# A hybrid decoder block: four instead of three k pairs by seven products in the second groups of two down parts

## The chip, the core and the metric

The kernel runs on one core of one Trainium2 chip. The core has a matrix engine (PE, with a separate weight-load stage PEld), a vector engine (DVE), an activation engine (ACT), a general engine (POOL) and a queue engine for transfers (SP). Each engine works through its own instructions in the order in which they stand; between engines only semaphores order anything. Weights come from the chip's memory by transfers that SP issues, and some by transfers that POOL issues and that add to what already lies in the buffer.

The metric is the device time of one execution in microseconds (us).

## The reference

One decoder layer over 256 tokens of width 2048 in float32: a Griffin branch and a stick-breaking attention side by side, a gated merge, then a SwiGLU feed-forward part and a gated per-layer embedding. Only the feed-forward part is touched here:

```python
h = rmsnorm(x, g_ffn[i])
gu = h @ w_ffn_gu[i]
g, u = jnp.split(gu, 2, axis=-1)
x = x + (jax.nn.silu(g) * u) @ w_ffn_down[i]
```

`w_ffn_gu` is 2048 by 11264 and `w_ffn_down` 5632 by 2048. The change concerns the last product, the down projection.

## The kernel before

**Products.** Everything is computed in float32 quality from operands that are split into a high and a low part of a format that the matrix engine takes. One product of a 128x128 token tile with a 128x512 weight tile is therefore three matmuls (high by high, high by low, low by high), written out in `prod` (L656; its matmuls are L658, L659, L660). The 256 tokens are two tiles. Weights are split after they have landed: ACT writes the high part `whi` (L374), DVE the low part `wlo` (L375). There are five buffers for each (pool `phl`, L432), so that a piece of weights can be split only when PE is through with the piece five places before it.

**Stages.** The feed-forward part runs as 11 gate-up groups `gu` (L1258) and three down parts `dn0`, `dn1`, `dn2` (`down`, L1291), interleaved: gu 0 to 3, dn0, gu 4 to 7, dn1, gu 8 to 10, dn2. A down part takes the k tiles that the groups before it have made (16, 16 and 12 of the 44) and has two groups, g = 0 and g = 1, one for each half of the 2048 output columns. Each group is two column blocks of 512 by two token tiles, and each adds its result onto the residual `x1`. Both groups of a part use the same tokens: the gated activations `acts`, one buffer for each pair of k tiles.

**Seven products for eight.** Two neighbouring k tiles (a pair), two token tiles and two column blocks make a 2x2 by 2x2 block product. Done plainly, it takes eight products (four for each k tile, an integer in the slot list). Done by Winograd's form of Strassen's scheme it takes seven, at the price of sums of weights and sums of tokens. The slot lists at L25 to L34 fix in which order the pieces of a group come. The first two such pairs share slots with string names ("11", "T1", "21", "T2", "22", "T3", "T4"); a third and a fourth pair have slots of their own, `A1`..`A4` = ("S", i, 2) and `B1`..`B4` = ("S", i, 3). `EVEN3` has three pairs by seven products and ten k tiles plainly; `EVEN4` has four pairs and eight k tiles plainly:

```python
EVEN3 = ["11", A1, 6, "T1", A2, 7, "21", 8, "T2", 9, "22", A3, 10, "T3", 11, A4, 12, "T4", 13, 14, 15]
EVEN4 = ["11", A1, 8, B1, "T1", 9, A2, B2, 10, "21", "T2", 11, "22", A3, 12, B3, "T3", 13, A4, B4, 14, "T4", 15]
```

`products` (L66) says how many products a slot has: four for an integer, two for a string name and for i = 1, 2, 3 of a third or fourth pair, one for i = 4. The gate-up groups (except the first) run `EVEN4`, dn0 and dn1 run `EVEN3` in both groups, dn2 has a list of its own.

**Sums of weights.** `Stream.summed` (L291) makes them on DVE (L296) just before a piece is split. For a third or fourth pair the piece ("S", 2) needs two adds of 128x512 into a new buffer, called Y here: Y's left half is the sum of a half of the pair's S1 buffer and a half of its S2 buffer, Y's right half is that plus the other half of S2. The piece "T2" needs one add of 128x1024, of the raw piece "22" into the running sum R. Other sums are made by POOL's adding transfers (`joins`, L330; L334). The raw pieces lie in 128x1024 buffers of the pool "Q" (31 of them, L437), from which the activations, the token sums and the norm-scaled inputs come as well; the plain k tiles have four buffers of their own (`p32`).

**Sums of tokens.** `half_sums` (L662) makes four sums of a pair's quarters on DVE (128x128 each) and splits them into a Q buffer (ACT copy, DVE subtract); with `defer` the split is put on a list that `group` runs at a slot. For gu outputs this is done in `turn` (L1270) while the pair is turned. Which pairs get sums is decided by `pairs_of` (L53): three for dn0 and dn1, so pairs 0 to 2 and 8 to 10. `parts_sums` (L970) makes the sums of a pair later, from its high and low parts; the value inputs of the attention and the attention output use it.

**Order.** `group` (L729) writes the products slot by slot, keeps a running time (0.68 for a product) at which `run_todo` starts work that was put off, such as the adds onto `x1` (`ends_x1` and `onto_x1`, L1188 to L1202), and calls `also[n]` at slot n. `Stream.need` (L387) lets the transfers, the splits and the sums run ahead. The order of the transfers on SP is planned by `dma_order` (L223) from the slot lists. After that a scheduler places each engine's instructions, and the pool gives out the buffers in the order of the program; a transfer or a sum that writes a buffer waits for the last reader of what lay in it before.

Of the kernel before, what the change touches and what calls it, by code (L numbers as in the profile page):

```python
# [29 lines left out]
FQ = [16, 16, 12]  # L30
FQ0 = [0, 16, 32]
# [4 lines left out]
EVEN3 = ["11", A1, 6, "T1", A2, 7, "21", 8, "T2", 9, "22", A3, 10, "T3", 11, A4, 12, "T4", 13, 14, 15]  # L36
EVEN4 = ["11", A1, 8, B1, "T1", 9, A2, B2, 10, "21", "T2", 11, "22", A3, 12, B3, "T3", 13, A4, B4, 14, "T4", 15]
LONG = ["11", 8, A1, 9, B1, "T1", 10, A2, 11, B2, "T2", 12, "21", 13, "22", A3, 14, B3, "T3", 15, A4, 16, B4, 17, "T4",
        18, 19, 20, 21]
TWELVE = [("S", 1, 0), ("S", 1, 1), 4, ("S", 2, 0), 5, ("S", 2, 1), 6, ("S", 3, 0), 7, ("S", 3, 1), 8, ("S", 4, 0), 9,  # L40
          ("S", 4, 1), 10, 11]
# [126 lines left out]
def tail():  # L168


    def wide(name, w, slots, c=0):
        return [(name, g, w, c + 8 * g, c + 8 * g + 4, slots[g]) for g in range(2)]

    def blocks(*cs):
        return [("blk", b, None, c, None, None) for c, b in cs]

    def gu(*gs):
        return [("gu", g, "gu", 4 * g, 44 + 4 * g, EVEN4 if g else FIRST3) for g in gs]

    def dn(q):  # L180
        k, p = FQ0[q], FQ0[q] // 2
        slots = [x + k if isinstance(x, int) else (*x[:2], x[2] + p) if isinstance(x, tuple) else x
                 for x in (EVEN3 if FQ[q] == 16 else TWELVE)]
        return wide(f"dn{q}", "dn", [slots] * 2)

    x = [("x", 0), ("x", 1)]
    return (wide("ro", "ro", [LONG] * 2) + wide("v", "in", [EVEN4] * 2, C_V)
            + [("qk", b, "in", C_Q + 4 * b, C_K + 4 * b, EVEN4) for b in range(2)]
            + blocks(*[(c, b) for b in (2, 3) for c in (C_Q, C_K)], *[(C_GTA, b) for b in range(4)])
            + wide("ao", "ao", [EVEN3] * 2) + wide("wo", "wo", [FIRST3, EVEN3]) + gu(0, 1, 2, 3) + dn(0) + gu(4, 5, 6, 7) + dn(1)  # L190
            + gu(8, 9, 10) + dn(2)
            + wide("pg", "pg", [FIRST3[:-4] + x + FIRST3[-4:]] * 2))
# [234 lines left out]
def tile_hybrid_block(ctx: ExitStack, tc: tile.TileContext, xT: bass.AP, x: bass.AP, pT: bass.AP,  # L427
# [12 lines left out]
    def tl(tag, dt=F32):  # L440
        cnt[0] += 1
        tag = "H" if tag in "CT" else "Q"
        n, c = NT[tag]
        return act.tile([P, c], dt, tag=tag, name=f"{tag}_{cnt[0]}", bufs=n)
# [217 lines left out]
    def half_sums(h, defer=False):  # L662


        a11, a21, a12, a22 = (h[:, c * P:c * P + P] for c in range(4))
        q = tl("T")
        s1, s2, s3, s4 = (q[:, c * P:c * P + P] for c in range(4))
        tt(s1, a21, a22, ALU.subtract)
        tt(s2, s1, a11, ALU.subtract)
        tt(s3, a11, a21, ALU.subtract)  # L670
        tt(s4, a12, s2, ALU.add)
        t = tl("X", F32R)

        def in_parts():
            actv(t[:, :512], q, AF.Copy)
            tt(t[:, 512:], q, f32(t[:, :512]), ALU.subtract)

        if defer:
            deferred.append(in_parts)
        else:  # L680
            in_parts()
        return [(t[:, c * P:c * P + P], t[:, 512 + c * P:640 + c * P]) for c in range(4)]
# [46 lines left out]
    def group(at, pairs, sums, after=None, also=()):  # L729

        name, g = at
        slots = [x for n, y, _, _, _, sl in HEAD + TAIL if (n, y) == at for x in sl
                 if isinstance(x, int) or is_sum(x)]
        turned_at = TURNED_AT["twelve" if len(slots) == len(TWELVE) else
                              "first" if slots[2] == 6 and slots[8] == "22" else "even"]  # L740
        seq = [(n, q, 0, 512) for n, x in enumerate(slots) for q in products(x, pairs_of(name)[:2])]
        if at == LAST_GROUP:
            k = len(slots) - 4
            rest = [q for q in seq if q[0] >= k]
            seq = [q for q in seq if q[0] < k] + [q for b in "243" for q in rest if q[1][0] == b]
            seq += [(n, (b + f, *q), e, e + 256) for e, f in ((0, "a"), (256, "b")) for n, (b, *q), _, _ in rest
                    if b == "8"]
        first, last = {}, {}
        for i, (_, (b, y, _, _), e, _) in enumerate(seq):
            first.setdefault(b, i)  # L750
            last[b, e] = i
            if y in ("11", "T1", "T2", "T3"):
                last[y] = i
        banks, tile_, got = {}, {}, {}
        begin = [0.0]
        for x in slots:
            begin.append(begin[-1] + 0.68 * len(products(x)))
        turns = list(turned_at)
        for i, (n, (b, y, p, c), e0, e1) in enumerate(seq):
            if n not in got:  # L760
                if n in also:
                    also[n]()
                run_todo(begin[n])
                while deferred:
                    with behind_splits():
                        deferred.pop(0)()
                if pend and turns and n >= turns[0] and not any(x[2] for x in todo):
                    turns.pop(0)
                    with tc.issue_after(mm_.ins):
                        pend.pop(0)()  # L770
                got[n] = S_.take(("tok", name, g, slots[n]))
            if b not in banks:
                banks[b] = psum()
            ps = banks[b]
            if p is None:
                o = tok(pairs, *y)
            else:
                o = {"11": tok(pairs, 2 * p, 0), "21": tok(pairs, 2 * p + 1, 0), "22": sums[p][3],
                     "T1": sums[p][0], "T2": sums[p][1], "T3": sums[p][2],
                     "T4": tok(pairs, 2 * p + 1, 1)}[y]  # L780
            _, _, hi, lo, w0 = got[n].columns(c)
            s = slice(w0 + e0, w0 + e1)
            mm_ = prod(ps[:, e0:e1], o, hi[:, s], lo[:, s], i == first[b], i in (last[b, e0], last.get(y)),
                 b == "B")
            if y in ("11", "T1", "T2", "T3") and i == last[y]:
                t = tile_[y] = tl("T")
                with tc.issue_after(S_.hi_ins.ins):
                    actv(t, ps, AF.Copy)
                if y == "T3":
                    with tc.issue_after(S_.lo_ins.ins):  # L790
                        tt(tile_["T2"], tile_["T1"], tile_["T2"], ALU.subtract)
                        tt(tile_["T1"], tile_["T1"], t, ALU.subtract)
                    if after is not None:
                        after(tile_, begin[n])
        run_todo(1e9)
        tile_["ends"] = [banks[b] for b in ("8a", "8b") if b in banks]
        return [banks[b] for b in "2438"], tile_
# [105 lines left out]
    @contextmanager  # L903
    def behind_splits():
        with tc.issue_after(S_.hi_ins.ins), tc.issue_after(S_.lo_ins.ins):
            yield
# [11 lines left out]
    also = {max(1, 2 * i - 4): [later(next_xg)] for i in range(2, NPD)}  # L918
    for i in range(NPD):
        also.setdefault(2 * i + 1 if i < 7 else 14, []).append(squares_x(i))  # L920
    also = {n: (lambda fs: lambda: [f() for f in fs])(fs) for n, fs in also.items()}
# [45 lines left out]
            later_on(a if tied else 0.0, (lambda c, q: lambda: tt(c, q, c, ALU.add))(c, q), True, tied)  # L967
        return cs

    def parts_sums(pairs, sums, p):  # L970
        h = tl("T")
        hi, lo = parts(pairs[p])
        tt(pair(h), f32(hi), f32(lo), ALU.add)
        sums[p] = half_sums(h)

    def last_gate():
        with behind_splits():
# [7 lines left out]
    for g in range(2):  # L985
        also = {n - 4 + i: (lambda p: lambda: parts_sums(xg, xsum, p))(p) for i, p in enumerate(pairs_of("v"))} if g else {
            8: last_gate, 12: next_table}
# [200 lines left out]
    def onto_x1(g):  # L1188

        def run(tiles, at):  # L1190
            for n, c in enumerate(("11", "T3", "T2", "T1")):
                o = x1[n % 2][2 * g + n // 2]
                later_on(at + 1.3 + 2.7 * n, (lambda o, t: lambda: tt(o, o, t, ALU.add))(o, tiles[c]), False)
        return run

    def ends_x1(pss, g, i):

        for n, ps in enumerate(pss):
            t, b = n % 2, 2 * g + n // 2
            later_on(max(0.0, JOINS_AT[n] - 1.3), (lambda o, ps: lambda: tt(o, ps, o, ALU.add))(x1[t][b], ps), True, n > 1)  # L1200
            if i is not None:
                later_on(6.8 + 2.7 * n, (lambda t, b: lambda: squares(i, t, b))(t, b), False)  # L1202
# [52 lines left out]
    acts, asum = {}, {}  # L1255
# [32 lines left out]
        pend.extend(turn(f) for f in range(2))  # L1288

    def down(q, g):  # L1290
        ends_x1(group((f"dn{q}", g), acts, asum, onto_x1(g))[0], g, 1 if q == 2 else None)  # L1291
        if q == 2:
            for p in range(4 * g, 4 * g + 4):
                pend.append(next_h(h3, sum3, p, PC_GP))
# [114 lines left out]
```

## Time and profile before

| | before |
|---|---|
| median of 3 runs (us) | 1850.68 (1850.08 to 1850.79) |
| profiled execution (us) | 1850.56 |
| its span (us) | 1848.9 |
| PE busy in the span | 1839.4 us, 99% |
| DVE busy | 1536.1 us, 83% |
| ACT busy | 1269.5 us, 69% |
| granted PE clock | full (1.0) |

The profile's first part gives for each engine the time in which it was busy. PE's busy time is modelled: matmuls overlap, so a row's duration (0.39 us for 128x512) is longer than the step from one matmul to the next. Idle time of PE is time in which it stood for want of an operand. In the lists, a row names a source line, an engine, an operation and the tiles (out<-in); "idle before" is how long the engine had nothing to do ahead of it, and the name behind the arrow is what ended that. The lines of helpers stand for many places: L374 and L375 are every split of a piece of weights, L454 and L460 are DVE's and ACT's general helpers.

### The profile page before, as it was taken

The page shows a single profiled execution, that of the slowest core. Times are in us where ns is not written, and L with a number is a line of the kernel's source. Part 1 is how long each engine was busy: PE and PEld are TensorE (multiplying, and loading weights), DVE is VectorE, ACT ScalarE, POOL GpSimd, SP SyncE. Part 2 cuts the span into 40 slices and gives each one's busy share as a digit, 9 for nine tenths or more (in the row PEclk, how much of TensorE's full clock was granted, in tenths as well). Part 3 has the DMA queues.
Part 4 walks back from the last instruction along what each step waited for, and adds up shares of the span by engine and source line. Part 5 has one row for each costly group of instructions (what it writes and reads, how often), then busy time and mean ns, then how long its engine had stood idle before and what let it go on. Part 6 is the DMA issues. An engine that isn't in the chain of part 4 may idle for free.

```text
span 1848.9 us, 24803 instructions
## 1 busy us (share of the span) xinstructions
PE 1839.4 (99%) x8855; PEld 1547.3 (84%) x8855; DVE 1536.1 (83%) x1940; ACT 1269.5 (69%) x1705; POOL 129.5 (7%) x156
## 2 busy tenths in 40 slices
PE   9999999999999999999999999999999999999998
PEld 7899899888888888888888888888888888888787
DVE  7688888677899977667799889888899888898987
ACT  7587888775566777776656686665566665666675
POOL 0000000010011100000000011100111101111100
PEclk9999999999999999999999999999999999999999
DMA  8555556587788855456788778888888888887774
GB/s 291 181 177 186 185 195 194 199 257 247 243 259 237 250 176 168 152 160 218 232 239 256 222 245 247 249 252 239 265 255 251 229 241 245 253 259 225 206 249 131
DMA packets 123388, 414.37 MB, mean 224 GB/s; under 512 B 13824, under 2 KB 14464, under 8 KB 123264
## 3 DMA queue, kind: packets, MB, share of 16 engines
q1 hardware_dynamic: 101808, 359.82, 55.5%
q0 software_dynamic: 21312, 52.96, 17.0%
q8 instruction: 69, 1.13, 0.2%
q14 instruction: 55, 0.45, 0.1%
q10 hardware_dynamic: 144, 0.01, 0.0%
HBM read 410.64 MB, written 2.10 MB: 223 GB/s over the span
## 4 chain that ended last, share of the span: by engine, by line
PE 97%; DVE 2%; issue 0%; ACT 0%; ACTq 0%
PE ps L658 26%; PE ps L659 26%; PE ps L660 26%; PE ps L576 9%; PE ps L580 5%; PE ps L559 1%; PE ps L560 1%; PE ps L558 1%; DVE wlo L375 1%; DVE H L454 1%; PE ps L1277 1%; PE ps L1035 0%; DVE Q L296 0%; PE ps L1222 0%; PE ps L495 0%
## 5 line engine op out<-in xcount | busy, mean ns | idle before, releaser
L659 PE MATMUL ps<-wlo,Q 128*128 128x512 f32 x2175 | 848.8, 390 | 1.3 <-DVE wlo L375 1.3
L660 PE MATMUL ps<-whi,Q 128*128 128x512 f32 x2175 | 845.7, 389 | 0.0
L658 PE MATMUL ps<-whi,Q 128*128 128x512 f32 x2175 | 751.5, 391 | 0.6 <-ACT whi L374 0.4
L375 DVE TENSOR_TENSOR wlo<-w,whi 128x1024 fp32r<-128x1024 f32 (+2 forms) x478 | 575.3, 1208 | 172.3 <-ACT whi L374 167.8
L374 ACT ACTIVATE whi<-w 128x1024 fp32r<-128x1024 f32 (+2 forms) x478 | 497.4, 1047 | 216.1 <-PE ps L660 168.1
L374 ACT ACTIVATE whi<-Q 128x1024 fp32r<-128x1024 f32 (+1 forms) x377 | 376.6, 1004 | 231.2 <-PE ps L660 184.3
L375 DVE TENSOR_TENSOR wlo<-Q,whi 128x1024 fp32r<-128x1024 f32 (+1 forms) x377 | 432.3, 1156 | 70.2 <-ACT whi L374 66.9
L659 PEld LDWEIGHTS ps<-wlo,Q 128*128 128x128 f32 x2175 | 408.8, 188 | 84.7 <-DVE wlo L375 2.2
L658 PEld LDWEIGHTS ps<-whi,Q 128*128 128x128 f32 x2175 | 408.1, 188 | 85.0 <-ACT whi L374 1.9
L660 PEld LDWEIGHTS ps<-whi,Q 128*128 128x128 f32 x2175 | 408.5, 188 | 84.3
L334 POOL DMA_DIRECT2D Q<-in_w_dram x148 | 126.8, 863 | 1668.9 <-PE ps L660 638.3
L576 PE MATMUL ps<-Q,whi 128*128 128x512 f32 x704 | 170.7, 392 | 0.0
L576 PEld LDWEIGHTS ps<-Q,whi 128*128 128x128 f32 x704 | 128.7, 188 | 24.5
L296 DVE TENSOR_TENSOR Q<-Q,Q 128x512 f32<-128x512 f32 (+1 forms) x148 | 128.2, 882 | 10.5 <-DMA Q<-in_w_dram 10.2
L460 ACT ACTIVATE H<-ps 128x512 f32<-128x512 f32 (+1 forms) x179 | 94.0, 539 | 45.7 <-PE ps L660 35.4
L454 DVE TENSOR_TENSOR H<-H,H 128x512 f32<-128x512 f32 (+2 forms) x214 | 120.2, 573 | 2.2 <-ACT H L460 1.0
L454 DVE TENSOR_TENSOR H<-ps,H 128x512 f32<-128x512 f32 (+1 forms) x162 | 96.3, 610 | 11.8 <-PE ps L660 7.2
L580 PEld LDWEIGHTS ps<-Q,wlo 128*128 128x128 f32 x704 | 90.4, 191 | 3.5
L580 PE MATMUL ps<-Q,wlo 128*128 128x256 f32 x704 | 91.5, 283 | 0.0
L460 ACT ACTIVATE Q<-H 128x512 fp32r<-128x512 f32 x70 | 43.2, 626 | 38.0 <-DVE H L454 37.4
L460 ACT ACT_TABLE_LOAD x52 | 66.7, 1283 | 3.1 <-DVE Q L454 2.2
L454 DVE TENSOR_TENSOR Q<-H,Q 128x512 fp32r<-128x512 f32 (+1 forms) x78 | 53.2, 686 | 1.4 <-ACT Q L460 1.4
(125 smaller groups left out, 896.7 us busy)
## 6 DMA issues: line engine op xcount, KB each, us to landing
w<-in_w_dram SPq DMA_DIRECT2D x453, 512.0 KB, 4.2
Q<-in_w_dram SPq DMA_DIRECT2D x202, 512.0 KB, 5.9
Q<-in_w_dram POOLq DMA_DIRECT2D x54, 512.0 KB, 7.1
Q<-in_w_dram POOLq DMA_DIRECT2D x94, 256.0 KB, 5.5
w<-in_w_dram SPq DMA_DIRECT2D x16, 448.0 KB, 3.4
H<-in_x_dram SPq DMA_DIRECT2D x8, 256.0 KB, 5.9
H<-in_xT_dram SPq DMA_DIRECT2D x7, 256.0 KB, 5.3
out_dram<-H SPq DMA_DIRECT2D x7, 256.0 KB, 2.6
```

What stands on the lines that cost most here:

```text
L296: add = lambda o, a, b: self.nc.vector.tensor_tensor(o, a, b, ALU.add)
L334: self.nc.gpsimd.dma_start(t[:, c:], src[:, a:a + 1024 - c], accum_op=ALU.add)
L374: self.hi_ins = self.nc.scalar.activation(h[:, q], t[:, q], AF.Copy)
L375: self.lo_ins = self.nc.vector.tensor_tensor(l[:, q], t[:, q], h[:, q].bitcast(F32), ALU.subtract)
L454: nc.vector.tensor_tensor(o, a, b, op)
L460: nc.scalar.activation(o, i, f, **kw)
L558: nc.tensor.matmul(o, wt[0], xh, start=start, stop=False)
L576: nc.tensor.matmul(pss[e], wt[0], rhs(xs, k), start=(k == 0), stop=(k == n - 1))
L580: nc.tensor.matmul(pss[e][:, :256], wt[1], rhs(xs, k)[:, :256], start=False, stop=False)
L658: nc.tensor.matmul(ps, x[0], wh, start=start, stop=False, skip_group_check=goes_on)
L659: nc.tensor.matmul(ps, x[0], wl, start=False, stop=False, skip_group_check=goes_on)
L660: return nc.tensor.matmul(ps, x[1], wh, start=False, stop=stop, skip_group_check=goes_on)
```

## The change

The slot list of the second group (g = 1) of dn0 and dn1 becomes `EVEN4`. The first groups keep `EVEN3`, and dn2 keeps its list. The fourth pair (pair 3 in dn0, pair 11 in dn1) therefore needs token sums; they are not made when the pair is turned, but late in the first group, at its slot 17 ("T4"), by `parts_sums` from the pair's parts, with the split put off until the work that is due at that slot has been issued. `parts_sums` gets the argument for that.

```diff
     def dn(q):
         k, p = FQ0[q], FQ0[q] // 2
-        slots = [x + k if isinstance(x, int) else (*x[:2], x[2] + p) if isinstance(x, tuple) else x
-                 for x in (EVEN3 if FQ[q] == 16 else TWELVE)]
-        return wide(f"dn{q}", "dn", [slots] * 2)
+        return wide(f"dn{q}", "dn", [
+            [x + k if isinstance(x, int) else (*x[:2], x[2] + p) if isinstance(x, tuple) else x for x in slots]
+            for slots in ((EVEN3, EVEN4) if FQ[q] == 16 else (TWELVE, TWELVE))])
...
-    def parts_sums(pairs, sums, p):
+    def parts_sums(pairs, sums, p, defer=False):
         h = tl("T")
         hi, lo = parts(pairs[p])
         tt(pair(h), f32(hi), f32(lo), ALU.add)
-        sums[p] = half_sums(h)
+        sums[p] = half_sums(h, defer)
...
     def down(q, g):
-        ends_x1(group((f"dn{q}", g), acts, asum, onto_x1(g))[0], g, 1 if q == 2 else None)
+        def fourth(p=FQ0[q] // 2 + 3):
+            with behind_splits():
+                parts_sums(acts, asum, p, True)
+
+        also = {len(EVEN3) - 4: fourth} if g == 0 and FQ[q] == 16 else {}
+        ends_x1(group((f"dn{q}", g), acts, asum, onto_x1(g), also)[0], g, 1 if q == 2 else None)
```

## The prediction

> **What bounds the kernel now.** I read the page first, then who waits for whom on PE, then the busy times stretch by stretch, then the timelines of PE, SP and DVE around the end of dn0's first group.
>
> ```profile
> span 1848.9 us, 24803 instructions
> PE 1839.4 (99%) x8855; PEld 1547.3 (84%) x8855; DVE 1536.1 (83%) x1940; ACT 1269.5 (69%) x1705; POOL 129.5 (7%) x156
> PE 97%; DVE 2%; issue 0%; ACT 0%; ACTq 0%
> ```
>
> PE is the bound, and 97% of the chain that ended last is PE. The waits of PE (us in total, times, longest):
>
> ```profile
> PE ps L495 <- DVE H L492: 1.6, 1, 1.6
> PE ps L659 <- DVE wlo L375: 1.3, 1, 1.3
> PE ps L658 <- ACT whi L374: 0.4, 1, 0.4
> ```
>
> The first is the start; only 1.7 us in all are waits for weights, none in a down part. So each product removed is worth its whole PE time, and each wait put in front of PE is lost in full. Busy time by stretch (PE, PEld, DVE, ACT, POOL, clock, DMA share, GB/s): a gate-up group with four pairs, dn0's first group, dn0's second, dn1's second:
>
> ```profile
> 1095.00:1137.00 42.00, 42.00 (x191) 34.75 (x190) 40.20 (x52) 30.62 (x36) 6.49 (x8) 1.00 0.87 261
> 1221.00:1263.00 42.00, 42.00 (x191) 34.76 (x190) 37.19 (x41) 25.55 (x29) 3.42 (x4) 1.00 0.82 240
> 1263.00:1305.00 42.00, 42.00 (x187) 34.79 (x186) 32.95 (x36) 23.71 (x26) 3.44 (x4) 1.00 0.80 249
> 1514.00:1556.00 42.00, 42.00 (x187) 34.79 (x186) 33.40 (x35) 24.10 (x26) 4.26 (x5) 1.00 0.79 250
> ```
>
> PE has no gap in any of them, and DVE can carry 40.2 of 42 us without making one.
>
> **What it removes.** A product is three matmuls:
>
> ```profile
> 1241.60 0.60 PE L1277 MATMUL ps<-ident,H 128*128 128x128 f32 x4
> ...
> 1241.95 0.48 PE L658 MATMUL ps<-whi,Q 128*128 128x512 f32 x1
> ...
> 1248.87 0.39 PE L658 MATMUL ps<-whi,Q 128*128 128x512 f32 x1
> 1249.55 0.39 PE L658 MATMUL ps<-whi,Q 128*128 128x512 f32 x1
> ```
>
> From one L658 to the next are 0.68 us for three matmuls, 0.227 each. `EVEN3` has 61 products, `EVEN4` 60: one product in each of two groups, six matmuls, 2 x 0.68 = 1.36 us. That is the whole possible gain, 0.07%; a measurement of this kernel tells about 0.2%, 3.7 us, from no change.
>
> **What it adds on DVE and ACT, and what hides it.** The durations (the last row is of a timeline, start and us ahead):
>
> ```profile
> L375 DVE TENSOR_TENSOR wlo<-Q,whi 128x1024 fp32r<-128x1024 f32 x20 | 24.5, 1223 | 6.5 <-ACT whi L374 6.2
> L374 ACT ACTIVATE whi<-Q 128x1024 fp32r<-128x1024 f32 x21 | 22.3, 1060 | 18.4 <-PE ps L660 18.4
> L460 ACT ACTIVATE H<-ps 128x512 f32<-128x512 f32 x8 | 4.7, 593 | 2.6 <-PE ps L660 2.6
> L296 DVE TENSOR_TENSOR Q<-Q,Q 128x1024 f32<-128x1024 f32 x4 | 4.9, 1220 | 0.0
> L296 DVE TENSOR_TENSOR Q<-Q,Q 128x512 f32<-128x512 f32 x5 | 3.4, 688 | 1.2 <-DMA Q<-in_w_dram 1.2
> L375 DVE TENSOR_TENSOR wlo<-Q,whi 128x512 fp32r<-128x512 f32 x2 | 1.4, 688 | 0.0
> 1115.69 0.31 DVE L454 TENSOR_TENSOR H<-H,H 128x128 f32<-128x128 f32 x1
> ```
>
> First group: the pair's parts are added (128x512, taken as the 0.69 of such rows), four sums of 128x128 (0.31 each), a subtract (0.69): 2.6 us of DVE, and one ACT copy, 0.59. The stretch then holds 37.2 + 2.6 = 39.8 of 42 us, under the 40.2 that makes no gap. The sums are wanted by `B2`, 18 products into the second group; in the program as built DVE finishes them three split pieces ahead. I cost them at nothing; without that cover they would cost up to 2.6 us.
>
> Second group: two plain pieces give way to three of 1024 and one of 512, +1.22 + 0.69 on DVE and about +1.06 + 0.6 on ACT, and two adds of 0.69: DVE 32.95 + 3.3 = 36.3 of 41.3 us, as loaded as gate-up groups are. POOL issues two more adding transfers. By the sums of busy time nothing is lost; what matters is where the new adds stand and which buffers they wait for.
>
> **Where it loses: the buffers.** In the program as built, all 31 Q buffers are in use when the second group's "22" is loaded: 12 hold the inputs of the gate-up groups still to come, then the activations, now four token sums instead of three, and the raw sums of two pairs instead of one. So two things wait that did not before. (a) B's new buffer Y (two adds of 0.69) takes the buffer of the activation pair of k tiles 8 and 9; its first add waits for the last matmul of k 9, the slot just ahead of `A2`, `B2`. (b) The load of "22", issued well ahead before, takes B's S1 buffer and is issued by SP only when that first add has read it. DVE then comes to T2's add, which needs "22", and stops there; behind it stand the low parts of k 10, "21" and T2. On ACT, behind B2's high part, stand the copy that frees a PSUM bank for `A2`, then the high parts of k 10, "21" and T2.
>
> The times, on the clock of before's trace. The four transposes at 1241.60 stand at slot 11 of the first group, 30 of its 61 products done. PE resumes at about 1242.0, so the second group starts at 1242.0 + 31 x 0.68 = 1263.1. Sixteen products (11, A1, 8, B1, T1, 9) end PE's part of k 9 at 1274.0; as a matmul's row is 0.39 and not 0.23 long, its buffer is free at 1274.2.
>
> Stall 1: adds 0.6 + 0.69 to 1275.5, B2's high part 1.06 to 1276.6. As built, PE does three matmuls of `A2` and then wants it, at 1274.7: 1.9 us lost. The next matmul wants the bank that ACT's copy (0.59, behind that high part) frees: 0.3 more. 2.2 us.
>
> Stall 2: "22" is issued at 1274.9, after the first add. What a load takes to land:
>
> ```profile
> w<-in_w_dram SPq DMA_DIRECT2D x453, 512.0 KB, 4.2
> Q<-in_w_dram SPq DMA_DIRECT2D x202, 512.0 KB, 5.9
> ...
> Q<-in_w_dram SPq DMA_DIRECT2D x14, 512.0 KB, 6.3
> ```
>
> (The last row is of 1220 to 1310 us alone.) The Q loads of before come in twos and threes behind others; this one comes alone, some 4 us behind the one ahead, as most w loads do. I take 5.0, nearer the w row, with ends 4.2 and 6.3. It lands at 1279.9; T2's add 1.22 to 1281.1, its high part 1.06 to 1282.2. As built, PE's first matmul of T2 comes 16 matmuls after k 9, in the midst of k 10: 1274.0 + 3.6 + 2.2 = 1279.8. Lost: 2.4 us (1.6 to 3.7).
>
> The rows give 4.2 to 6.3 us for a load of 512 KB. [...]
>
> Sum: 2.2 + 2.4 - 0.68 = 3.9 us lost for each part (3.1 to 5.2). dn1 has the same instructions in the same order with the same buffers waiting, 250 us later: 7.8 (6.2 to 10.4). Elsewhere the streams differ only in gu 4 and gu 8, where a few adds move, and in the last stage, where a few splits change places by one or two; that stage has the 1.3 us wait of L659, so -1.3 to +1.3, taken as 0. On the profiled execution: 1850.56 + 7.8 = 1858.4; the median shown is 0.12 higher: **1858.5**.
>
> **The rivals.**
>
> *Cover holds, only the products are gained:* 1850.68 - 1.36 = 1849.3, not slower. It needs k 9's buffer and "22" to be no later than PE; for it speaks that four-pair groups run without a gap today (first stretch above), against it that there Q has room and "22" is loaded early. Chance 0.08.
>
> *Only stall 1:* "22" lands within the time that stall 1 gives. 2 x (2.2 - 0.68) = +3.0: 1853.7. It would need about 2.6 us to land; a Q row of 5.9 speaks against it, a quiet queue at that moment for it. Chance 0.12.
>
> *It spreads:* the next gate-up group begins late on its own S2 loads. In gu 4 DVE waits for them already:
>
> ```profile
> 1302.51 0.69 DVE L296 TENSOR_TENSOR Q<-Q,Q 128x512 f32<-128x512 f32 x1 [0.65 <-DMA Q<-in_w_dram]
> 1303.76 0.69 DVE L296 TENSOR_TENSOR Q<-Q,Q 128x512 f32<-128x512 f32 x1 [0.56 <-DMA Q<-in_w_dram]
> ```
>
> As built, these adds now stand a place or two earlier on DVE, ahead of low parts that PE needs; each such wait, with one add, would cost PE some 1.3 us, twice in each of two groups at most: 1858.5 + 2.6 to 5.2, say 1862. Against it: PE comes later too, and I find about 1 us of room. Chance 0.15.
>
> *The clock:* PE standing still lowers its granted clock. The stretch in which PE idles most shows it:
>
> ```profile
> 1835.00:1849.00 14.00, 7.86 (x47) 6.79 (x45) 7.79 (x15) 3.08 (x5) 0.00 (x0) 0.95 0.21 75
> ```
>
> 0.95 over 14 us is 0.7 us lost; once a part that is +1.4: 1859.9. Against it: the 1.3 us wait left the slices of the page at full clock. Chance 0.04. [...]
>
> That the change does not do what it says is out: the program as built has six matmuls fewer.
>
> **How the numbers follow.** The forecast, both stalls in both parts, has 0.61, with its own range 1856.9 to 1861.1. Faster by over 0.2% would need three times the whole gain: 0.01. Within 0.2% (to 1854.4) lie the first rival, most of the second, and little else: 0.16. Slower: 0.83. The range that should hold 8 in 10 goes from 1853 to 1863: it takes in the second rival and the middle of the spreading one.
>
> **What would show it.** In the profile after: PE's waits of about 2 us for `whi` L374 and of about 2 to 3 us for `whi` L374 behind L296, once each about 11 to 17 us into the second groups of dn0 and dn1; before the longer one a wait of DVE L296 for a transfer of several us, before the shorter one a DVE wait for PE L660. The token sums show no PE wait in the first groups. If PE's waits for weights stay near 1.7 us in all, the buffers were not the limit and I am wrong; if DVE's wait at T2's add is under 2 us, the landing was mis-sized.

## The result and the profile after

| | before | after |
|---|---|---|
| median (us) | 1850.62 (1850.03 to 1851.20, 6 runs) | 1864.63 (1860.33 to 1867.14, 6 runs) |
| ratio to before | | 1.0075 (95%: 1.0065 to 1.0086) |
| profiled execution, its span (us) | 1850.56, 1848.9 | 1865.39, 1863.7 |

The change makes the kernel 14 us slower; 7.8 were forecast, and 1853 to 1863 was the range. Times here and below leave out three executions of 2784 to 3303 us in later runs, one of them of the kernel before. First PE's waits for weights in the profile after (us in total, times, longest):

```profile
PE ps L658 <- ACT whi L374: 11.6, 6, 4.7
PE ps L659 <- DVE wlo L375: 1.3, 1, 1.3
```

The other waits are as before. The first of these was 0.4 us, once, and is now 11.6. Where these waits stand, from PE's timeline of dn0's and then dn1's second group (start, us, in brackets the idle time before and what ended it):

```profile
1276.66 0.98 PE L658 MATMUL ps<-whi,Q 128*128 128x512 f32 x2 [1.99 <-ACT whi L374]
1284.85 0.80 PE L658 MATMUL ps<-whi,Q 128*128 128x512 f32 x1 [4.69 <-ACT whi L374]
...
1535.60 0.99 PE L658 MATMUL ps<-whi,Q 128*128 128x512 f32 x2 [1.99 <-ACT whi L374]
1541.42 0.50 PE L658 MATMUL ps<-whi,Q 128*128 128x512 f32 x1 [2.32 <-ACT whi L374]
```

Two gaps in each part: the first equal in both, the second twice as long in dn0. What stands behind them on DVE, in the same two groups:

```profile
1274.02 1.42 DVE L296 TENSOR_TENSOR Q<-Q,Q 128x512 f32<-128x512 f32 x2 [0.23 <-PE ps L660]
1282.39 1.23 DVE L296 TENSOR_TENSOR Q<-Q,Q 128x1024 f32<-128x1024 f32 x1 [4.53 <-DMA Q<-in_w_dram]
...
1532.96 1.42 DVE L296 TENSOR_TENSOR Q<-Q,Q 128x512 f32<-128x512 f32 x2 [0.24 <-PE ps L660]
1538.97 1.23 DVE L296 TENSOR_TENSOR Q<-Q,Q 128x1024 f32<-128x1024 f32 x1 [2.17 <-DMA Q<-in_w_dram]
```

The rows of 128x512 are Y's two adds of pair B: they begin when PE has read k 9's activations for the last time. The rows of 128x1024 are T2's add: it waits for the load of "22". SP issued that load right behind Y's first add, and it took from issue to landing (the view of transfers, first dn0, then dn1; the row has the durations of the issue in ns, and first and last start):

```profile
L285 SPq DMA_DIRECT2D Q<-in_w_dram x1: 328/328/328, 1274.8 to 1274.8; - x1
...
DMA to landing us min/median/max: 7.6/7.6/7.6
...
L285 SPq DMA_DIRECT2D Q<-in_w_dram x1: 327/327/327, 1533.7 to 1533.7; - x1
...
DMA to landing us min/median/max: 5.2/5.2/5.2
```

So the same load landed in 7.6 us in one part and 5.2 in the other. In both parts POOL issued two adding transfers within 0.7 us of it (POOL's timeline, dn0, then dn1):

```profile
1274.14 1.78 POOL L334 DMA_DIRECT2D Q<-in_w_dram  x2 [2.08 <-DVE wlo L375]
...
1533.08 1.78 POOL L334 DMA_DIRECT2D Q<-in_w_dram  x2 [2.07 <-DVE wlo L375]
```

By the program the first adds to A's buffer Y, which the kernel before has too, and the second to B's S2 buffer, which is new. A third loss does not show as a wait at all. PE's timeline behind the long gap in dn0, and the windows (PE, PEld, DVE, ACT, POOL, clock, DMA share, GB/s) of dn0's first group, of 3 us behind the second gap of each part, and of the last stage:

```profile
1285.44 0.63 PE L659 MATMUL ps<-wlo,Q 128*128 128x512 f32 x1
1285.87 0.63 PE L660 MATMUL ps<-whi,Q 128*128 128x512 f32 x1
```

```profile
1221.00:1263.00 42.00, 42.00 (x191) 34.76 (x190) 36.15 (x44) 26.08 (x30) 1.72 (x2) 1.00 0.75 231
1285.00:1288.00 3.00, 3.00 (x8) 2.33 (x8) 3.00 (x3) 2.17 (x3) 0.62 (x1) 0.50 0.52 174
1543.00:1546.00 3.00, 3.00 (x10) 2.39 (x9) 2.88 (x3) 1.38 (x2) 0.85 (x1) 0.63 0.58 164
1740.00:1800.00 60.00, 58.61 (x268) 47.41 (x267) 52.15 (x73) 46.63 (x76) 3.44 (x4) 1.00 0.71 219
```

From one matmul to the next are 0.43 us where the prediction had 0.227: PE is busy the whole time, at half its clock (0.50 and 0.63 granted, in each case until some 4 us after the gap). In dn0 the clock is low already before the gap ends: the spell of half clock lasts from 1282.39 to 1289.22. In dn1 it lasts from 1541.81 to 1545.22. The first group, where the token sums are made, has no gap, and the last stage has its full clock.

To see that nothing else was lost, take the four transposes of a turn near the start of dn0 and dn1 and behind each of them. Before (the row of 1241.60 stands in the prediction), then after:

```profile
1361.98 0.27 PE L1277 MATMUL ps<-ident,H 128*128 128x128 f32 x1
1487.98 0.60 PE L1277 MATMUL ps<-ident,H 128*128 128x128 f32 x4
1612.03 0.27 PE L1277 MATMUL ps<-ident,H 128*128 128x128 f32 x1
```

```profile
1241.38 0.60 PE L1277 MATMUL ps<-ident,H 128*128 128x128 f32 x4
1370.67 0.27 PE L1277 MATMUL ps<-ident,H 128*128 128x128 f32 x1
1496.67 0.60 PE L1277 MATMUL ps<-ident,H 128*128 128x128 f32 x4
1626.79 0.27 PE L1277 MATMUL ps<-ident,H 128*128 128x128 f32 x1
```

From the first to the second row dn0's stretch grew from 120.38 to 129.29 us, by 8.91; dn1's from 124.05 to 130.12, by 6.07; between them nothing changed (126.00 in both). Together 15.0, and the span grew by 14.8. By starts of matmuls against a step of 0.227, each part divides so:

| us | dn0 | dn1 | forecast |
|---|---|---|---|
| one product less | -0.68 | -0.68 | -0.68 |
| stall 1 (with the wait for a PSUM bank) | 2.53 | 2.53 | 2.2 |
| stall 2 | 4.85 | 2.47 | 2.4 (1.6 to 3.7) |
| matmuls at half clock | 2.16 | 1.73 | 0 |
| sum | 8.86 | 6.05 | 3.9 |

### The profile page after: what moved, and what is told of

Read it like the earlier page. It is cut to its first block, busy times and chain, and to the rows that moved or that the text cites. A ratio compares the mean times of both kernels' runs of the same rounds, so it can differ in the third digit from the quotient of the medians.

```text
span 1863.7 us, 24829 instructions
## 1 busy us (share of the span) xinstructions
PE 1843.0 (99%) x8849; PEld 1547.7 (83%) x8849; DVE 1545.9 (83%) x1960; ACT 1273.1 (68%) x1711; POOL 133.0 (7%) x160
## 4 chain that ended last, share of the span: by engine, by line
PE 96%; DVE 2%; DMA 1%; issue 0%; ACT 0%; SPq 0%; ACTq 0%
PE ps L659 26%; PE ps L660 26%; PE ps L658 26%; PE ps L576 9%; PE ps L580 5%; PE ps L559 1%; PE ps L560 1%; PE ps L558 1%; DMA Q<-in_w_dram 1%; DVE wlo L375 1%; DVE H L454 1%; DVE Q L296 1%; PE ps L1277 1%; PE ps L1035 0%; ACT whi L374 0%
## 5 line engine op out<-in xcount | busy, mean ns | idle before, releaser
L659 PE MATMUL ps<-wlo,Q 128*128 128x512 f32 x2173 | 849.9, 391 | 1.3 <-DVE wlo L375 1.3
L660 PE MATMUL ps<-whi,Q 128*128 128x512 f32 x2173 | 846.7, 390 | 0.0
L658 PE MATMUL ps<-whi,Q 128*128 128x512 f32 x2173 | 745.4, 392 | 11.8 <-ACT whi L374 11.6
L375 DVE TENSOR_TENSOR wlo<-w,whi 128x1024 fp32r<-128x1024 f32 (+2 forms) x474 | 569.9, 1207 | 167.8 <-ACT whi L374 163.4
L374 ACT ACTIVATE whi<-w 128x1024 fp32r<-128x1024 f32 (+2 forms) x474 | 493.4, 1047 | 208.4 <-PE ps L660 159.3
L374 ACT ACTIVATE whi<-Q 128x1024 fp32r<-128x1024 f32 (+1 forms) x385 | 383.9, 1003 | 251.1 <-PE ps L660 179.6
L375 DVE TENSOR_TENSOR wlo<-Q,whi 128x1024 fp32r<-128x1024 f32 (+1 forms) x385 | 440.7, 1153 | 75.1 <-ACT whi L374 71.9
L658 PEld LDWEIGHTS ps<-whi,Q 128*128 128x128 f32 x2173 | 408.1, 188 | 99.0 <-ACT whi L374 15.2
L659 PEld LDWEIGHTS ps<-wlo,Q 128*128 128x128 f32 x2173 | 409.1, 188 | 84.9 <-DVE wlo L375 2.5
L660 PEld LDWEIGHTS ps<-whi,Q 128*128 128x128 f32 x2173 | 409.1, 188 | 84.5
L334 POOL DMA_DIRECT2D Q<-in_w_dram x152 | 130.6, 864 | 1679.9 <-PE ps L660 675.6
L296 DVE TENSOR_TENSOR Q<-Q,Q 128x512 f32<-128x512 f32 (+1 forms) x152 | 130.7, 875 | 10.6 <-DMA Q<-in_w_dram 9.7
```

What stands on the lines that cost most here:

```text
L296: add = lambda o, a, b: self.nc.vector.tensor_tensor(o, a, b, ALU.add)
L334: self.nc.gpsimd.dma_start(t[:, c:], src[:, a:a + 1024 - c], accum_op=ALU.add)
L374: self.hi_ins = self.nc.scalar.activation(h[:, q], t[:, q], AF.Copy)
L375: self.lo_ins = self.nc.vector.tensor_tensor(l[:, q], t[:, q], h[:, q].bitcast(F32), ALU.subtract)
L658: nc.tensor.matmul(ps, x[0], wh, start=start, stop=False, skip_group_check=goes_on)
L659: nc.tensor.matmul(ps, x[0], wl, start=False, stop=False, skip_group_check=goes_on)
```

## The experiments

Theory: the second groups lack buffers (Y waits for k 9's, the load of "22" waits for Y), and the gaps then lower the clock. Rival 1: the work added on DVE and ACT. Rival 2: the token sums made late. In the kernels whose edit adds a line near the top, L659, L375, L376, L297 and so on are the L658, L374, L375, L296 of the other rows.

**1. Another order of the second groups.** The slot list alone is changed:

```diff
+DOWN4 = ["11", 8, A1, 9, B1, "T1", 10, A2, B2, 11, "21", 12, "T2", "22", A3, B3, "T3", 13, A4, B4, 14, "T4", 15]
...
-            for slots in ((EVEN3, EVEN4) if FQ[q] == 16 else (TWELVE, TWELVE))])
+            for slots in ((EVEN3, DOWN4) if FQ[q] == 16 else (TWELVE, TWELVE))])
```

> The changed kernel with another order of the second groups, nothing else: 11, 8, A1, 9, B1, T1, 10, A2, B2, 11, 21, 12, T2, 22, A3, B3, T3, 13, A4, B4, 14, T4, 15 (as many products, sums and loads as in the change). k 8 and 9 now end 22 and 14 products ahead of B2 instead of 10 and 4, and T2 comes 28 products behind k 9 where it was 12. Theory (the buffers: Y waits for k 9's buffer, the load of 22 waits for Y, and after the two gaps the clock is halved): Y's buffer is free long before Y is wanted, 22 is issued about 10 us before T2 is wanted, both stalls and the half clock are gone, 1849.3 (1848.5 to 1851.0). Rival 1 (the added work of DVE and ACT, 3.3 and 1.7 us a part, is what PE waits for): the loss stays, 1860 to 1865. Rival 2 (the token sums made late are the cause): the loss stays as well, 1860 to 1865.

Measured: 1848.99 us (1848.36 to 1849.64, 10 runs) against 1850.43, ratio 0.9992 (0.9982 to 1.0001). DVE's L297 rows and PE's busy time and clock in dn0's and dn1's second group:

```profile
1270.76 2.17 DVE L297 TENSOR_TENSOR Q<-Q,Q 128x512 f32<-128x512 f32 x3
1279.24 1.22 DVE L297 TENSOR_TENSOR Q<-Q,Q 128x1024 f32<-128x1024 f32 x1
```

```profile
1263.00:1303.00 40.00, 40.00 (x178) 33.14 (x177) 35.30 (x40) 24.71 (x27) 6.01 (x7) 1.00 0.87 260
1514.00:1554.00 40.00, 40.00 (x178) 33.12 (x177) 35.30 (x38) 23.64 (x26) 6.90 (x9) 1.00 0.91 274
```

PE has no gap in either and its full clock. No add waits, neither for PE nor for a transfer, although all the added sums, splits and late token sums are there. That takes rivals 1 and 2 out for this loss: the same work in another order loses nothing. (The interval reaches 1; the gain itself is taken up in experiment 10.)

**2. The late token sums alone.**

```diff
-            for slots in ((EVEN3, EVEN4) if FQ[q] == 16 else (TWELVE, TWELVE))])
+            for slots in ((EVEN3, EVEN3) if FQ[q] == 16 else (TWELVE, TWELVE))])
```

> The fourth pair's token sums are made late in the first groups as in the change, but the second groups keep three pairs by seven products; the fourth sums are read by nothing. Theory (buffers): the sums are hidden, and one more buffer held matters little without Y and B's raw pieces: 1850.6 (1850 to 1852). Rival 1 (added work in the second group): 1850.6 as well. Rival 2 (the late sums): most of the loss of 14 is here, 1860 to 1865.

Measured: 1850.16 (1849.96 to 1851.42), ratio 0.9999 (0.9989 to 1.0008). The sums are hidden, as the forecast had it; rival 2 is out by this run too.

**3 and 4. One more buffer, and its control.** The change, and the kernel before, with this line:

```diff
-    NT = {"Q": (31, 1024), "H": (18, 512)}
+    NT = {"Q": (32, 1024), "H": (16, 512)}
```

> The changed kernel with 32 buffers in Q instead of 31, paid for by 16 instead of 18 of the small ones (H). As built, Y then takes a free buffer and its adds stand right behind A's; the load of 22 still takes B's S1 buffer and so still waits for Y's first add, which comes some 2.5 us earlier. Theory: stall 1 (2.5 us a part) is gone; stall 2 stays at 1 to 4 us a part; with one gap in place of two close together the clock stays up or falls once. 1849.3 + 2 x (1 to 4) = 1851 to 1858, and in the profile no wait of DVE L296 for PE. Rival 1 (added work): 1860 to 1865, as the change. Rival 2 (late sums): 1860 to 1865.

> The kernel before with 32 and 16 buffers, the control of the run with one more buffer: what the fewer small buffers cost by themselves. All theories: 1850.6 (1849.5 to 1852.5), unless the small buffers are short somewhere, which would then have to be taken off the other run too.

Measured: 1849.98 (1849.20 to 1851.56) with the change, 1850.63 (1849.73 to 1852.48) without, both against 1850.43. The one buffer is worth 14.6 us to the change and nothing to the kernel before. Of the change with it, DVE's adds and SP's issue of "22" with its landing, in dn0:

```profile
1270.17 2.74 DVE L296 TENSOR_TENSOR Q<-Q,Q 128x512 f32<-128x512 f32 x4
1277.83 1.22 DVE L296 TENSOR_TENSOR Q<-Q,Q 128x1024 f32<-128x1024 f32 x1
```

```profile
L285 SPq DMA_DIRECT2D Q<-in_w_dram x1: 328/328/328, 1272.2 to 1272.2; - x1
...
DMA to landing us min/median/max: 4.6/4.6/4.6
```

Y's four adds (A's and B's) run in one go; "22" goes out 2.5 us sooner and is there by 1276.9, before DVE reaches T2's add. I had expected 1 to 4 us of stall 2 to stay in each part, for this load still takes B's S1 buffer; none stayed. So in this run the two stalls go together: with Y in time, "22" is in time.

**5. Gaps made on purpose.** In the kernel before, PE is made to stand in eight gate-up groups; `GAPS` says at which slot and how long:

```diff
+    def still(m, n):
+        ps, t = psum(), tl("T")
+        with tc.issue_after(m.ins):
+            nc.tensor.transpose(ps[:, :P], ident, ident)
+        for _ in range(n):
+            actv(t[:, :P], t[:, :P] if _ else ps[:, :P], AF.Copy)
+        m = nc.tensor.transpose(ps[:, P:2 * P], t[:, :P], ident)
+        return m
...
+                if n in GAPS.get(at, {}):
+                    gap = still(mm_, GAPS[at][n])
...
-            mm_ = prod(ps[:, e0:e1], o, hi[:, s], lo[:, s], i == first[b], i in (last[b, e0], last.get(y)),
-                 b == "B")
+            with tc.issue_after(gap.ins) if gap else nullcontext():
+                mm_ = prod(ps[:, e0:e1], o, hi[:, s], lo[:, s], i == first[b], i in (last[b, e0], last.get(y)),
+                     b == "B")
```

> The kernel before with PE made to stand in eight gate-up groups: PE transposes a constant, ACT copies the result and then copies it on n times, PE transposes the copy, and only then go the products on. Single gaps of about 1.7 to 5.6 us (n = 2 shortest, n = 10 longest) in gu 1, 2, 3, 5, 6, 7, 9, and in gu 10 a pair, about 2.0 and 2.3 us with some 4 us of products between, as in dn1 of the change. Read by the granted clock in the 3 us behind each gap. Theory A (one gap is enough, from a length between 1.3, which did nothing in before, and 2.3 us, which lowered it in dn1): the clock falls behind every single gap of 2.3 us and more. Theory B (it is the idle share of some microseconds together): a single gap of 2.0 to 2.8 leaves the clock at 1.0, the pair lowers it. [...]

Two of the gaps in PE's timeline, and the windows of 3 us behind them:

```profile
1476.55 0.33 PE L736 MATMUL ps<-ident,H 128*128 128x128 f32 x1 [3.25 <-ACT H L461]
1688.65 0.33 PE L736 MATMUL ps<-ident,H 128*128 128x128 f32 x1 [1.89 <-ACT H L461]
```

```profile
1476.60:1479.60 3.00, 3.00 (x14) 2.50 (x15) 1.50 (x3) 1.30 (x2) 0.86 (x1) 1.00 0.84 299
1688.70:1691.70 3.00, 3.00 (x10) 2.40 (x11) 0.68 (x2) 0.63 (x1) 0.00 (x0) 0.71 0.99 384
```

The clock fell behind 1.89, 2.23, 2.48, 2.57 and 4.27 us and did not behind 0.78, 1.20, 1.54 and, against theory A, 3.25. All the ends of the slow spells, where the step goes from 0.43 back to 0.23, lie on one grid of 3.41 us, to 0.06; the granted clocks of the windows of 3 us at these gaps put its changes on that grid too, to 0.05 (0.60 in 1214.90 to 1217.90, so 0.50 from 1215.50 on). On it the 3.25 us divide into 1.61 and 1.64, while the 1.89 lie in one stretch.

**6. POOL's transfers postponed.** The adding transfer into Y was put four pieces later in the program:

```diff
-                self.joins(self.raw[g(("Y", mode[2]))], 512, g(("S", 1, mode[2])), 512)
+                self.held.append((self.n_split + (4 if g(0)[0] in ("dn0", "dn1") and g(0)[1] == 1 else 0), lambda g=g, mode=mode: self.joins(
+                    self.raw[g(("Y", mode[2]))], 512, g(("S", 1, mode[2])), 512)))
+            while self.held and self.held[0][0] <= self.n_split:
+                self.held.pop(0)[1]()
```

> The changed kernel, but in the second groups the adding transfers of POOL that are issued when A2 and B2 have been split (one each, 256 KB) are issued four pieces later, so that none of them stands in front of the load of 22. Nothing is left out. Theory (the load of 22 landed 7.6 us late in dn0 and not 5.2, as in dn1, because POOL's transfers went out at the same moment): 22 lands in 4.5 to 5.5 us in both parts, stall 2 is 1.7 to 2.6 us in both, dn0 loses about 6 as dn1 does: 1860 to 1862.5. Rival (the landing varies for other reasons, or PE waits for something else): no change, 1863 to 1867.

Measured: 1865.38 to 1869.31, ratio 1.009 (1.0074 to 1.0105). It decides nothing: the scheduler issued POOL's two transfers just ahead of "22" as in the change (at 1275.06, with "22" at 1275.70). As a repetition it shows how the landing varies: 6.3 us in dn0 and 6.0 in dn1.

**7. Gaps once more, twenty of them.** The kernel of experiment 5 with another table of gaps, to test the grid.

> As the first run with gaps, with two single gaps of 1.2 to 4 us in each of gu 1 to 10, twenty in all. In the first such run the clock fell behind gaps of 1.89, 2.23, 2.48, 2.57 and 4.27 us, and did not behind 0.78, 1.20, 1.54 and 3.25. All its changes of step between 0.43 and 0.23 lie on a grid of 3.41 us. Theory (the clock is set in fixed stretches of 3.41 us: half for the stretch that follows one in which PE stood for more than half, 1.7 us): with the grid read off this run's own changes, every gap of which more than 1.7 us lie in one stretch is followed by a stretch at half clock, and no other is, whatever its length; none under 1.7 us, most but not all of 1.9 to 3.3. Rival (a limit on the gap's length, some 1.7 us, and the 3.25 an accident of another kind): all gaps above 1.8 are followed by half clock at once. [...]

Four of the gaps, and what followed:

```profile
1130.09 0.33 PE L736 MATMUL ps<-ident,H 128*128 128x128 f32 x1 [2.23 <-ACT H L461]
1158.87 0.33 PE L736 MATMUL ps<-ident,H 128*128 128x128 f32 x1 [2.23 <-ACT H L461]
1206.45 0.33 PE L736 MATMUL ps<-ident,H 128*128 128x128 f32 x1 [2.96 <-ACT H L461]
1682.66 0.33 PE L736 MATMUL ps<-ident,H 128*128 128x128 f32 x1 [1.88 <-ACT H L461]
```

```profile
1130.10:1133.10 3.00, 3.00 (x8) 2.44 (x9) 0.61 (x2) 0.10 (x1) 0.00 (x0) 0.54 0.51 186
1158.90:1161.90 3.00, 3.00 (x14) 2.48 (x15) 0.59 (x2) 1.66 (x2) 0.50 (x1) 1.00 0.74 147
1206.50:1209.50 3.00, 3.00 (x14) 2.49 (x15) 0.89 (x2) 1.66 (x2) 0.75 (x1) 1.00 0.86 202
1682.70:1685.70 3.00, 3.00 (x9) 2.45 (x10) 0.92 (x2) 0.46 (x1) 0.00 (x0) 0.60 0.49 139
```

Two gaps of 2.23 us, one followed by half clock and one not; 2.96 not, 1.88 yes. So the length does not decide, and the rival is out. On the grid on which this run's granted clock changes, the six gaps that lowered the clock have 1.88, 2.03, 2.15, 2.23, 2.24 and 2.27 us in one stretch; the fourteen that did not have 1.67 and less, but for three with 1.77, 1.80 and 1.92. Those three miss the theory's border of 1.7, and no other border puts it right, since 1.92 left the clock alone and 1.88 did not: in between both happen, and why is open.

The theory lacks one thing more. Behind a gap of 3.25 us that ends at 1629.76 the half clock lasts for two stretches of the grid:

```profile
1625.25:1628.66 3.41, 1.26 (x7) 0.75 (x5) 1.82 (x2) 2.58 (x6) 0.00 (x0) 1.00 0.67 261
1628.67:1632.08 3.41, 2.32 (x6) 1.93 (x7) 0.69 (x2) 0.94 (x4) 0.00 (x0) 0.50 0.62 203
1632.08:1635.49 3.41, 3.41 (x9) 2.64 (x8) 1.85 (x4) 1.55 (x2) 0.57 (x1) 0.50 0.63 258
```

PE stood for 2.15 us of the first stretch. In the second, already at half clock, it stood for 1.09, and the third was at half clock too. The gap that ends at 1660.27 did the same with 0.88; where a slow stretch held 0.53 us of idling or less, the next one was at full clock.

**8. Without four of POOL's transfers in each part.** The two calls of `joins` for pieces ("S", 2), of A and of B, are left out in the second groups of dn0 and dn1; their sums are then missing from the result:

```diff
-                self.joins(b, 512, g(("S", 2, p)), 0)
+                if at not in ([x, 1] for x in ("dn0", "dn1")):
+                    self.joins(b, 512, g(("S", 2, p)), 0)
...
-            elif isinstance(mode, tuple) and mode[:2] == ("S", 2):
+            elif isinstance(mode, tuple) and mode[:2] == ("S", 2) and PLAN[i][0][1:3] not in (("dn0", 1), ("dn1", 1)):
```

> The changed kernel without four of POOL's adding transfers in the second group of dn0 and dn1 (256 KB each: those that add to A's and B's S2 buffers and Y buffers; these sums are left out of the result). Two of them go out within 1 us of the load of 22 in the change. The earlier attempt to postpone them left POOL's order as it was, so this question is still open. Theory (these transfers make 22 land later than the 4.6 us of the run with 32 buffers): 22 lands in 4 to 5 us in both parts, stall 2 falls to 1.0 to 2.0 us, the time to 1856 to 1860. Rival (22 lands as it does for the loads of SP ahead of it and the chip's memory): 5 to 7.6 us as before, 1862 to 1867.

Measured: 1856.59 to 1857.52, ratio 1.0035 (1.0021 to 1.0048). The landing of "22" in dn0 and dn1, and PE's gaps:

```profile
DMA to landing us min/median/max: 3.4/3.4/3.4
...
DMA to landing us min/median/max: 3.5/3.5/3.5
```

```profile
1277.06 1.28 PE L659 MATMUL ps<-whi,Q 128*128 128x512 f32 x2 [1.99 <-ACT whi L375]
...
1530.47 0.98 PE L659 MATMUL ps<-whi,Q 128*128 128x512 f32 x2 [1.98 <-ACT whi L375]
1534.57 0.50 PE L659 MATMUL ps<-whi,Q 128*128 128x512 f32 x1 [0.60 <-ACT whi L375]
```

Without the four transfers of each part the load lands in 3.4 and 3.5 us, even sooner than expected; of stall 2, 0.6 us is left in one part, and stall 1 is as it was. So most of stall 2 comes from these transfers. Which of the four do it was not separated: two go out beside the load, one 3.6 us before and one 3.7 behind it. Nor do they explain why it took 7.6 us in dn0 and 5.2 in dn1, where POOL issued them at the same distances. The run is also stall 1 by itself: it lowers the clock in dn0 (the two matmuls of the row at 1277.06 take 1.28 us, those of the equal gap in dn1 0.98), and not in dn1. On the grid of this run's granted clock the gap lies whole in one stretch in dn0, and in dn1 it is divided into 1.46 and 0.52. The sum holds: 1850.5 - 1.36 + 2 x 2.53 + 0.75 + 1.6 (eight matmuls at 0.43 in place of 0.227, 1277 to 1280.7) = 1856.6.

**9. Four pairs in both groups.** The order of experiment 1 in both groups, sums of four pairs made at the turn, 32 and 16 buffers:

```diff
-        return [FQ0[q] // 2 + i for i in range(3 if FQ[q] == 16 else 2)]
+        return [FQ0[q] // 2 + i for i in range(4 if FQ[q] == 16 else 2)]
...
-            for slots in ((EVEN3, EVEN4) if FQ[q] == 16 else (TWELVE, TWELVE))])
+            for slots in ((DOWN4, DOWN4) if FQ[q] == 16 else (TWELVE, TWELVE))])
...
-        also = {len(EVEN3) - 4: fourth} if g == 0 and FQ[q] == 16 else {}
+        also = {}
```

> What the theory offers as a better kernel: the order of the first experiment in both groups of dn0 and dn1 (four pairs by seven products in each), token sums of four pairs made where the pairs are turned, 32 buffers in Q and 16 in H. Twelve matmuls fewer than before, 2.7 us. Theory: no waits of over 0.5 us in the down parts, 1847.5 to 1849.0. Rival 1 (DVE's added work, here in the first groups too, is too much): 1850 to 1856. If the buffers are short in spite of the extra one, a wait for whi or wlo of 1 to 4 us in the second groups: 1850 to 1858.

Measured: 1849.63 (1847.91 to 1851.52, 11 runs) against 1850.34, ratio 0.9996 (0.9987 to 1.0005). The median lies above the 1847.5 to 1849.0 expected. The down parts have only one wait, of 0.4 us, so the buffers are not short. In the profiled execution (1850.46) the gain is given back at the start of the last stage:

```profile
1748.84 0.50 PE L659 MATMUL ps<-whi,Q 128*128 128x512 f32 x1 [0.38 <-ACT whi L375]
1750.60 0.55 PE L660 MATMUL ps<-wlo,Q 128*128 128x512 f32 x1 [1.27 <-DVE wlo L376]
```

```profile
1740.00:1800.00 60.00, 58.36 (x257) 47.59 (x256) 49.43 (x60) 41.17 (x58) 6.03 (x7) 0.97 0.73 215
```

The wait of 1.27 us that every version has here left the clock alone in the change; with another of 0.38 half a microsecond ahead of it the clock is halved, 0.03 of 60 us, 1.8. (The two are 1.65 us of idling in one stretch, less than the 1.92 of a single gap that left the clock alone in experiment 7; whether two gaps count for more than one was not tested.) The fastest run, 1847.91, is what twelve matmuls less would give (1850.34 - 2.72 = 1847.6). That the other runs differ by the same cause is not shown, for only one execution has a profile.

**10. The kernel of experiment 1, measured again.**

> The first experiment's kernel once more, against the kernel before in more rounds, as the version that may beat both: 1849.0 (1848.3 to 1849.7), 1.4 us below before, which is the 1.36 us of the six matmuls.

Measured: 1849.02 (1848.67 to 1849.80, 11 runs) against 1850.50, ratio 0.9992 (0.9983 to 1.0002). The interval just reaches 1, but both runs of this kernel give 1.4 to 1.5 us less than before, which is the 1.36 us of the six matmuls, and 1849.80, the slowest of its 21 executions, stands at the fastest of before (1849.76, with experiment 1). It beats the change by 15.6 us. In both runs every execution lies below every one of the kernel before that was taken with it, so a gain of about the size that the change was to bring is likely, though neither interval leaves out 1.

## Why the prediction was right about the stalls and wrong in its sum

- **PE is the bound, a product is 0.68 us:** right. Where the stalls are gone, six matmuls less are 1.4 us less (experiments 1 and 10).
- **The late token sums cost nothing:** right; no PE wait in the first group's window, and 1850.16 with them alone.
- **DVE's and ACT's added work is hidden:** right; it is all there in experiment 1.
- **Stall 1:** right in place and cause (PE waits for `whi`, DVE's adds for PE L660), 2.53 for 2.2 us. One buffer more removes it.
- **Stall 2:** right in place and cause (T2's add waits for "22", issued behind Y's first add at 1274.8 for 1274.9). In dn1 5.2 us to land and 2.47 lost, for 5.0 and 2.4. In dn0 the term was mis-sized: 7.6 to land, beyond my end of 6.3, and 4.85 lost. I chose 5.0 because this load "comes alone" on SP. POOL's adding transfers, of which I named two more, I gave no price, and two go out within 0.7 us of this load; without the four of each part it lands in 3.4 (experiment 8). Why dn0's took longer than dn1's stays open, and that dn1 came out near 5.0 is in part luck.
- **"dn1 has the same instructions in the same order":** true, but not the same times: 8.9 and 6.1 us, for the landing differs.
- **The clock:** the step that failed most. I costed it at nothing, gave the rival 0.04 and a price of 0.7 us a part, and argued from the 1.3 us wait that leaves the clock alone. The price was misread: in the row of 0.95, all 7.86 us of PE's work lie before 1847.55, at a granted clock of 1.00, and the half clock behind it falls where PE has nothing left to do. The clock fell in both parts and cost 2.16 and 1.73 us. Gaps of the lengths that I had forecast, 2.2 and 2.4 us, can lower it: 2.23 and 2.48 us did in experiment 5, and 2.23 us in one place of experiment 7 and not in another. The wait that I argued from is shorter than any single gap that lowered it, the shortest of which took 1.77 us (experiment 6). Nor does the length decide alone: 1.88 us was enough in experiment 7, and 3.25 us was not in experiment 5, where two stretches of the grid shared it as 1.61 and 1.64.
- **Spreading into gu 4 and gu 8:** did not happen; nothing was lost outside the two parts.

Of the 7.0 us between the forecast loss and the one measured in the profile (14.8 - 7.8), the half clock is 3.9, stall 2 in dn0 2.5, and stall 1 0.7. So two terms failed: the clock, put at nothing, and the landing of "22", sized too small.

## What to carry to other kernels

When a pool is full, look at which last reader each new write will wait for, and then at which load waits for that write: one buffer or one changed order can be worth more than the work saved. Where PE will stand for about 2 us or more, ask what a stretch at half clock would add to the sum (1.6 to 2.2 us in a down part here). A load's landing is to be judged against all queues that send at that moment, those of the change included (here "22" took 5.2 and 7.6 us, and 3.4 and 3.5 without four of POOL's transfers in each part).

## What the runs showed of the hardware

In the profile of the change the granted clock changed at 1282.39, 1289.22, 1541.81 and 1545.22, on a grid of 3.41 us; the changes of experiments 5 and 7 lie on such a grid as well. In the profiles of the change and of experiments 5 to 8, every stretch of the feed-forward part in which PE stood for 1.96 us or more was followed by one at half clock (the shortest such times: 1.96 in experiment 5, 2.00 in 6, 2.03 in 7, 1.99 in 8); such a spell cost 1.6 to 2.2 us in the down parts. Behind a stretch at full clock in which a single gap took 1.67 us or less none came in experiment 7. In between both happened: 1.77, 1.80 and 1.92 did not lower the clock in experiment 7, while 1.88 did; in experiment 6, 1.94 did not and 1.77 did. Two gaps of 1.65 us together lowered it in experiment 9. A stretch that was itself at half clock was followed by another with as little as 0.88 us of idling in it (experiment 7).

Whether a gap of 1.9 to 3.3 us was followed by half clock went with where it fell on that grid: 2.23 us in one stretch and 2.23 us divided in experiment 7, 1.99 whole and 1.98 divided in experiment 8. If the gaps of the change fall on it differently in each execution, which is my estimate and was not shown, that fits the 6.8 us between the fastest and the slowest run of the change against 1.2 for before; that this is the whole of that spread was not shown either, for the landing of "22" varies as well.

The load of "22" (512 KB), with SP's next load 0.4 us behind it, landed in 3.4 and 3.5 us without four of POOL's adding transfers in each part (experiment 8), and with them in 4.6 (experiment 3, dn0), 5.2 and 7.6 (the change) and 6.0 and 6.3 (experiment 6).
